# The mixing product of a hybrid decoder block as seven products of quarters, in three passes, with its weights' sums made during the convolution's output product

## The chip, the cores and the metric

The kernel runs on one core of a Trainium2 chip. The core's engines are TensorE (PE in the profile: matrix products; PEld its loading of the stationary operand), VectorE (DVE), ScalarE (ACT), GpSimd (POOL) and SyncE (SP). All DMAs of this kernel are issued from SP's queue. The metric is the device time of one execution, in microseconds, as the median of several runs of the same program.

## The reference

One decoder block for 512 tokens of width 1024, all in float32. Two token mixers run beside each other, are weighted by gates and added, and go through a mixing product; a gated feed-forward network follows. Cut to what matters:

```python
h = rmsnorm(x, norm1_g)
z_glu, z_rx, z_rg, z_ga, z_gb = split(h @ w_in + b_in)
u = z_glu[..., :1024] * sigmoid(z_glu[..., 1024:])
u = silu(layernorm(causal_depthwise_conv(u, conv_dw_w, conv_dw_b)))
y_a = u @ conv_w_out + conv_b_out
hb = rg_lru(causal_depthwise_conv(z_rx, lru_conv_w, lru_conv_b), ...)
y_b = (hb * gelu(z_rg)) @ lru_w_out
m = sigmoid(z_ga) * y_a + sigmoid(z_gb) * y_b
x = x + m @ w_mix_out                  # the mixing product, 512 x 1024 x 1024
h = rmsnorm(x, norm2_g)
x = x + (silu(h @ ffn_w1) * (h @ ffn_w3)) @ ffn_w2     # inner width 2816
return rmsnorm(x, norm_f_g)
```

## The kernel before

Up to `m` the channels lie on the 128 partitions and the 512 tokens along the free dimension. From the mixing product on, tokens lie on the partitions: four token tiles of 128, each in two halves of 512 columns.

**Every product in three matmuls.** Operands are split into a high part, rounded to TensorE's fp32r format, and a low part, the remainder (`split_to`, L106): ScalarE writes the high part (a CAST, L108 in the profile), another engine subtracts (L104). A product is high x high + high x low + low x high: `mm3` (L310, matmuls at L319) for products with channels on the partitions, `token_mm` (L676, matmuls at L680) for the mixing product, and `product` (L789, matmuls at L794) for the last one.

**Weights.** All weights are streamed in the order of one list of chunks, written with `wchunk` (L121). A chunk of up to 128x1024 is loaded by SP into one of four slots (`raw`, `RAW = 4`) and split into one of five (`hl`, `HL = 5`); its low part is made by GpSimd for the input, LRU-output, convolution-output and mixing weights, and by VectorE for the feed-forward weights. `weights(key)` (L150) emits the program for the chunks up to four places beyond the one it returns (`AHEAD = 4`). A `raw` slot comes free when both parts are made, an `hl` slot when the last matmul that reads it is done.

**Order.** But for the start, the order on each engine is set by the framework's scheduler: it goes through the program with its own estimate of the times and gives each engine the earliest instruction in program order that is ready. A tile is placed when a slot of its kind is free. On the chip each engine then executes its list strictly in that order. SP's list too: a DMA that waits for its data or its slot holds up those behind it.

**The stages around the change**, in order of time:
1. `yb`: the LRU's output product, 8 column blocks; the gate `sgb` is multiplied in.
2. `ya`, the convolution's output product ("conv_out" below), 8 blocks of 24 matmuls with weights `co0` to `co7`. After each block VectorE adds the bias, multiplies the gate (L668), adds the LRU's share (L669), and splits the result into `m{j}` (512 columns).
3. `mx`, the mixing product: 8 row blocks of `w_mix_out`. The first four blocks (`mx0` to `mx3`) are multiplied for all 8 token-and-half combinations into 8 PSUM banks. The last four (`LAST = 4`) are kept in long-lived tiles, and `mix_rows(t)` (L703) finishes token tile after token tile: 24 matmuls, the residual `x2` added (L707), the sum of squares and its root (`rstd_of`, L330), the scaled rows `xs` (L711), and `x2` stored to DRAM (L712) for the end.
4. `turn_half(hf)` (L344): `xs` of two token tiles are turned by TensorE (16 transposes, `th`, L351), and copied as high parts `h2..h` by ScalarE (L354) and low parts `h2..l` by VectorE (L355). Half 0 is written in the program before `mix_rows(3)`, half 1 among the first FFN products.
5. `f`, the FFN: 22 pairs of products with `w1` and `w3` (4 chunks for two inner blocks); the first two blocks (`EARLY = 2`) are made token half by token half. `ffn_out` (L732) multiplies and, for each second block, makes the operands of the last product (`pair_out`, L744) and the sums of its weights (`weight_sums`, L757).
6. `r`, the last product, by Strassen's scheme in Winograd's form: the 512 x 2816 operand and the 2816 x 1024 weights are cut into quarters (256 tokens x 1408, 1408 x 512), and seven products of sums of quarters take the place of eight. The sums of the weights (`t1` to `t4`) are made once on VectorE from two 512 KB loads (`ws`) and stored to DRAM; they come back as chunks. Three passes over the inner blocks follow: A with products `r1`, `r2`, `r5`; B with `r7`, `r1` continued, and `r2` anew (named `r3`); C with `r1` continued. Between passes VectorE adds the banks into the four token tiles; `finish` normalises and stores rows.

The sums of the operands that the passes need are written by `pair_out` as `ua` (split at once), `s1p`, `ea` and `va` (both split late, in pass A).

Of the kernel before, what the change touches and what calls it, by code (L numbers as in the profile page):

```python
# [75 lines left out]
def tile_block(ctx, tc, a, out):  # L76
# [139 lines left out]
    KH = NF // 2  # L216
    PAIRED = [j for k in range(KH) for j in (k, k + KH)]
    for j in PAIRED:
# [4 lines left out]
    w2 = a["ffn_w2"][0].rearrange("(k p) n -> p k n", p=P)  # L223
    b11, b12, b21, b22 = (lambda k, i=i, h=h: w2[:, k + KH * i, h * T : (h + 1) * T] for i in range(2) for h in range(2))
    dram = ctx.enter_context(tc.tile_pool(name="dram", bufs=1, space=bass.MemoryType.DRAM))
    sums_ = {(n, k): dram.tile([P, T], F32, tag=f"{n}_{k}", name=f"{n}_{k}") for n in ("t1", "t2", "t3", "t4") for k in range(KH)}
    x2_kept = [[dram.tile([P, T], F32, tag=f"x2k{t}{h}", name=f"x2k{t}{h}") for h in range(2)] for t in range(NT)]

    def quarters(key, of):
        def load(raw):  # L230
            for i, q in enumerate(of):
                nc.sync.dma_start(raw[:, i * T : (i + 1) * T], q)

        wchunk(key, load, len(of), T, lo=vec)

    two = lambda q, k: [q(i) for i in (k, k + 1) if i < KH]
    kept = lambda n: lambda k: sums_[n, k][:, :]
    for n, q, m in (("A", [b11, kept("t1")], b21), ("B", [kept("t2"), kept("t3")], b22)):
        for k in range(KH):
            if k % 2 == 0:  # L240
                quarters(f"o{n}s{k}", two(m, k))
            quarters(f"o{n}{k}", [v(k) for v in q])
    for k in range(0, KH, 2):
        quarters(f"oC{k}", two(kept("t4"), k))
# [417 lines left out]
    m = []  # L662
    for j in range(8):
        ws = w_tiles(f"co{j}", ND)
        ps = bank(f"ya{j}")
        mm3(ps, ws, un)
        o = sga[j]
        vec.scalar_tensor_tensor(out=o, in0=ps, scalar=pc("conv_b_out", j), in1=o, op0=ALU.add, op1=ALU.mult)  # L668
# [4 lines left out]
    def token_banks(name):  # L673
        return [[(bank if t < 3 else bank2)(f"{name}{t}{h}") for h in range(2)] for t in range(NT)]

    def token_mm(po_, n_k, k, x_, w_, t, h):  # L676
        xh, xl = (v[:, t * P : (t + 1) * P] for v in x_[k])
        wh, wl = w_[h]
        for i, (l_, r_) in enumerate(((xh, wh), (xh, wl), (xl, wh))):
            pe.matmul(po_[t][h], l_, r_, start=k == 0 and i == 0, stop=k == n_k - 1 and i == 2)  # L680

    def w_halves(key):
        w_ = weights(key)
        if isinstance(w_, list):
            return w_
        return [tuple(v[:, 0, h * T : (h + 1) * T] for v in w_) for h in range(2)]
# [6 lines left out]
    pm = token_banks("mx")  # L693
    for k in range(8 - LAST):
        w_ = w_halves(f"mx{k}")
        for t in range(NT):
            for h in range(2):
                token_mm(pm, 8, k, m, w_, t, h)
    wm = [w_halves(f"mx{k}") for k in range(8 - LAST, 8)]
    h2p = [pairt(f"h2{c}") for c in range(ND)]  # L700
    xs = []

    def mix_rows(t):  # L703
        for h in range(2):
            for i in range(LAST):
                token_mm(pm, 8, 8 - LAST + i, m, wm[i], t, h)
            vec.tensor_tensor(out=x2[t][h], in0=pm[t][h], in1=x2[t][h], op=ALU.add)  # L707
        sc = [longt(f"xs{t}{h}") for h in range(2)]
        r = rstd_of(x2[t], sc)
        for h in range(2):  # L710
            vec.tensor_scalar(out=sc[h], in0=x2[t][h], scalar1=r, scalar2=None, op0=ALU.mult)  # L711
# [15 lines left out]
    add = lambda o, x, y: vec.tensor_tensor(out=o, in0=x, in1=y, op=ALU.add)  # L727
    LO, HI = HALVES
    ops = []
    uv = []  # L730

    def ffn_out(j, p1, p3):  # L732
# [3 lines left out]
        if i == 0:  # L736
            uv.append((longt(f"ua{k}"), longt(f"va{k}")))
        for dst, cs in zip(uv[k], HALVES):
            vec.tensor_tensor(out=dst[:, HALVES[i]], in0=s_[:, cs], in1=p3[:, cs], op=ALU.mult)  # L739
        if i:  # L740
            pair_out(k, *uv[k])
            weight_sums(k)
# [66 lines left out]
    for k in range(KH):  # L809
        if k % 2 == 0:  # L810
            m_ = pairs_of(f"oAs{k}")
# [115 lines left out]
```

## Time and profile before

| | |
|---|---|
| median of 3 runs | 823.18 us (822.99 to 823.85) |
| the profiled execution | 823.95 us, span 821.4 us |
| TensorE busy | 810.8 us (99%), 3774 matmuls |
| VectorE, ScalarE, GpSimd busy | 556.5, 412.3, 215.4 us |
| conv_out stage (`ya`) | 377.15 to 420.83 us |
| mixing product (`mx`), with the first turning | 420.83 to 466.36 us |
| FFN (`f`), with the second turning | 466.36 to 709.81 us |
| last product (`r`) | from 709.81 us |
| DMA | 122.96 MB, mean 150 GB/s |

How to read it: times in lists are in us from the span's start, and the second number is a duration. "x168" is a count. In square brackets or after "|" stands how long the engine was idle before, and what ended that. A matmul's own duration (0.39 us) is longer than the pitch at which matmuls follow each other. In tables by stage each engine's busy time is followed by its count of instructions, and the last three columns are the clock granted to TensorE, the share of time in which the DMA engines were busy, and what they moved. `hl_co`, `hl_mx`, `hl_f` are split weights of the convolution's output, the mixing product and the FFN, `raw_..` the loaded ones.

### The profile page before, as it was taken

The numbers are of one execution on the slowest core, as the hardware profiler recorded it, in microseconds if no ns is written. First come the engines' busy times: TensorE is split into PE (matmuls) and PEld (weight loads), VectorE is DVE, ScalarE is ACT, GpSimd is POOL, SyncE is SP. The second block draws the span as 40 slices with busy tenths as digits, with TensorE's granted clock in tenths as the row PEclk, the third lists the DMA queues.
The fourth block names the chain that finished last, engine by engine and source line by source line (L and its number), as shares of the span: only waits on it lengthen the run. The fifth ranks groups of instructions, "written<-read, shape, count | busy, mean of one in ns | idle before, by whom it ended". The sixth has DMA issues, their size and how long they took to land.

```text
span 821.4 us, 10487 instructions
## 1 busy us (share of the span) xinstructions
PE 810.8 (99%) x3774; PEld 678.1 (83%) x3774; DVE 556.5 (68%) x849; ACT 412.3 (50%) x574; POOL 215.4 (26%) x120
## 2 busy tenths in 40 slices
PE   8999999999999999999999999999999999999996
PEld 7988888888888888888888898888888888888885
DVE  4699999999989965723644546554554445688457
ACT  7545788768578565733234343222222222476434
POOL 3555446445434543365461000000000000000000
PEclk9999999999999999999999999999999999999999
DMA  7544434334333412244367218666666665786552
GB/s 214 160 116 103 116 92 117 97 104 122 103 90 103 119 48 81 81 150 139 98 196 220 77 44 266 203 204 177 184 193 201 194 205 195 243 275 207 182 167 103
DMA packets 154310, 122.96 MB, mean 150 GB/s; under 512 B 10919, under 2 KB 128083, under 8 KB 154259
## 3 DMA queue, kind: packets, MB, share of 16 engines
q1 hardware_dynamic: 154259, 122.31, 49.4%
q8 instruction: 29, 0.48, 0.2%
q14 instruction: 22, 0.18, 0.1%
HBM read 103.54 MB, written 15.73 MB: 145 GB/s over the span
## 4 chain that ended last, share of the span: by engine, by line
PE 97%; ACT 1%; DMA 1%; DVE 1%; issue 0%; SPq 0%; ACTq 0%
PE z L319 34%; PE f L319 29%; PE r L794 13%; PE yb L319 7%; PE mx L680 5%; PE ya L319 5%; PE g L590 3%; DMA raw_in<-in_w_in_dram 1%; PE th L351 0%; PE tx L351 0%; DVE x L366 0%; SPq L275 0%; DVE x2b L727 0%; DVE of L859 0%; ACT hl_in L108 0%
## 5 line engine op out<-in xcount | busy, mean ns | idle before, releaser
L469 DVE SCALAR_TENSOR_TENSOR cv<-u,par,cv 128x511 f32<-128x511 f32 (+17 forms) x240 | 162.7, 730 | 1.4 <-ACT cv L466 1.2
L104 POOL TENSOR_TENSOR hl_in<-raw_in,hl_in 128x1024 fp32r<-128x1024 f32 x52 | 125.5, 2417 | 135.7 <-ACT hl_in L108 122.2
L108 ACT CAST hl_f<-raw_f 128x1024 fp32r<-128x1024 f32 x44 | 46.3, 1053 | 149.3 <-PE f L319 83.1
L104 DVE TENSOR_TENSOR hl_f<-raw_f,hl_f 128x1024 fp32r<-128x1024 f32 x44 | 53.8, 1222 | 49.2 <-ACT hl_f L108 49.2
L108 ACT CAST hl_in<-raw_in 128x1024 fp32r<-128x1024 f32 x52 | 54.2, 1043 | 11.1 <-PE z L319 6.8
L739 DVE TENSOR_TENSOR ua<-si,f 128x256 f32<-128x256 f32 x22 | 9.3, 422 | 62.9 <-PE f L319 62.2
L319 PE MATMUL z<-h10h,hl_in 128*128 128x512 f32 (+1 forms) x112 | 42.2, 378 | 0.7 <-DVE h10l L355 0.7
L319 PE MATMUL z<-h11h,hl_in 128*128 128x512 f32 (+1 forms) x112 | 41.7, 374 | 0.0
L319 PE MATMUL z<-h17h,hl_in 128*128 128x512 f32 (+1 forms) x112 | 41.7, 374 | 0.0
L319 PE MATMUL z<-h14h,hl_in 128*128 128x512 f32 (+1 forms) x112 | 41.7, 374 | 0.0
L319 PE MATMUL z<-h15h,hl_in 128*128 128x512 f32 (+1 forms) x112 | 41.7, 374 | 0.0
L319 PE MATMUL z<-h13h,hl_in 128*128 128x512 f32 (+1 forms) x112 | 41.7, 374 | 0.0
L319 PE MATMUL z<-h16h,hl_in 128*128 128x512 f32 (+1 forms) x112 | 41.7, 374 | 0.0
L319 PE MATMUL z<-h12h,hl_in 128*128 128x512 f32 (+1 forms) x112 | 41.7, 374 | 0.0
L319 PE MATMUL f<-h22h,hl_f 128*128 128x512 f32 (+1 forms) x96 | 35.4, 371 | 0.0
L319 PE MATMUL f<-h25h,hl_f 128*128 128x512 f32 (+1 forms) x96 | 35.4, 372 | 0.0
L319 PE MATMUL f<-h23h,hl_f 128*128 128x512 f32 (+1 forms) x96 | 35.4, 372 | 0.0
L319 PE MATMUL f<-h26h,hl_f 128*128 128x512 f32 (+1 forms) x96 | 35.4, 372 | 0.0
L319 PE MATMUL f<-h24h,hl_f 128*128 128x512 f32 (+1 forms) x96 | 35.4, 371 | 0.0
L319 PE MATMUL f<-h27h,hl_f 128*128 128x512 f32 (+1 forms) x96 | 35.3, 371 | 0.0
L319 PE MATMUL f<-h20h,hl_f 128*128 128x512 f32 (+1 forms) x96 | 35.0, 373 | 0.3 <-ACT h20h L354 0.3
L319 PE MATMUL f<-h21h,hl_f 128*128 128x512 f32 (+1 forms) x96 | 35.3, 371 | 0.0
(815 smaller groups left out, 2252.1 us busy)
## 6 DMA issues: line engine op xcount, KB each, us to landing
raw_in<-in_w_in_dram SPq DMA_DIRECT2D x52, 512.0 KB
raw_f<-in_ffn_w_dram SPq DMA_DIRECT2D x44, 512.0 KB
ws<-in_ffn_w_dram SPq DMA_DIRECT2D x22, 512.0 KB
t<-ws SPq DMA_DIRECT2D x44, 256.0 KB
raw_oB<-t SPq DMA_DIRECT2D x22, 256.0 KB
raw_lo<-in_lru_w_out_dram SPq DMA_DIRECT2D x16, 320.0 KB
x<-in_x_dram SPq DMA_DIRECT2D x16, 256.0 KB
raw_co<-in_conv_w_out_dram SPq DMA_DIRECT2D x8, 512.0 KB
```

Source lines behind the costliest of these rows:

```text
L104: eng.tensor_tensor(out=o, in0=x, in1=y, op=ALU.subtract)
L108: copy(h, full)
L319: pe.matmul(ps, l, r, start=i == 0, stop=i == n - 1)
L469: vec.scalar_tensor_tensor(out=acc[c][:, s:], in0=u[c][:, : T - s], scalar=dw(c, s), in1=acc[c][:, s:], op0=ALU.mult, op1=ALU.add)
L590: pe.matmul(ps, l, r, start=k == 0, stop=k == len(mms) - 1)
L680: pe.matmul(po_[t][h], l_, r_, start=k == 0 and i == 0, stop=k == n_k - 1 and i == 2)
L739: vec.tensor_tensor(out=dst[:, HALVES[i]], in0=s_[:, cs], in1=p3[:, cs], op=ALU.mult)
L794: pe.matmul(banks[i], l_[:, ts], r_, start=start and n == 0, stop=stop and n == 2, skip_group_check=again)
```

## The change

The scheme of the last product is put into two classes, `Quartered` (the chunks) and `Sevenfold` (operands and passes), and used for both the mixing product (four inner blocks a quarter) and the last one (eleven).

- conv_out's blocks are made in the order 0, 4, 1, 5, 2, 6, 3, 7. Each result is added straight into `u`/`v` tiles (two half-width additions); the split of `m` is gone. After each second block `pair` makes and splits operands, and `weight_sums` loads two row blocks of `w_mix_out` (512 KB each), makes four sums on VectorE and stores them in DRAM.
- The mixing weights no longer come as eight chunks, four of them in long-lived tiles, but as 14 chunks of quarters and sums through the five `hl` slots (As0, A0, A1, As2, A2, A3, Bs0, B0, B1, Bs2, B2, B3, C0, C2, each of two 256 KB loads), with the low part made by VectorE. The first FFN chunks follow after them in the list.
- The product is three passes: A and B of 72 matmuls, C of 24. Token tiles 0 and 1 are complete after pass B and go through `norm2_rows` ahead of pass C in the program; then stand the sums of tiles 2 and 3, then pass C: its first two blocks for both tiles, the last two (`hold` = 2) for tile 2 with its norm, then for tile 3. Only then comes `turn_half(0)`.
- In the last product, `finish` of tiles 0 and 1 now stands right after their sums, ahead of the sums of tiles 2 and 3, instead of inside pass C; `hold` stays 3.

The core of the diff:

```diff
-    for j in range(8):
+    for j in [0, 4, 1, 5, 2, 6, 3, 7]:
         wchunk(f"co{j}", conv_out[:, :, j * P : (j + 1) * P], ND, P)
-    LAST = 4
-    mix = a["w_mix_out"][0].rearrange("(k p) (o n) -> p k o n", p=P, o=1)
-    for k in range(8):
-        wchunk(f"mx{k}", mix[:, k, :, :], 1, D, "hl" if k < 8 - LAST else "long")
+    class Quartered:
+        def __init__(self, name, w, kh, lo):
...
+            for n, q, m in (("A", [raw(0, 0), kept("t1")], raw(1, 0)), ("B", [kept("t2"), kept("t3")], raw(1, 1))):
+                for k in range(kh):
+                    if k % 2 == 0:
+                        chunk(f"{n}s{k}", two(m, k))
+                    chunk(f"{n}{k}", [v(k) for v in q])
+            for k in range(0, kh, 2):
+                chunk(f"C{k}", two(kept("t4"), k))
...
+    mixq = Quartered("mx", a["w_mix_out"][0].rearrange("(k p) n -> p k n", p=P), ND // 2, vec)
...
+    class Sevenfold:
...
+        def tile(self, j, make):
+            k, i = j % self.kh, j // self.kh
+            if i == 0:
+                self.uv.append((longt(f"{self.name}u{k}"), longt(f"{self.name}v{k}")))
+            for dst, cs in zip(self.uv[k], HALVES):
+                make(cs, dst[:, HALVES[i]])
+            if i:
+                self.pair(k, *self.uv[k])
+                self.weight_sums(k)
+        def pair(self, k, ua, va):
+            n = self.name
+            u_ = split(f"{n}us{k}", ua, vec)
+            s1 = shortt(f"{n}s1{k}")[:, LO]
+            add(s1, va[:, LO], va[:, HI])
+            sp = longt(f"{n}s1p{k}", F32R)
+            split_to(sp[:, LO], sp[:, HI], s1, vec)
+            e = longt(f"{n}e{k}")
+            sub(vec, e[:, HI], ua[:, LO], va[:, LO])
+            sub(vec, va[:, LO], s1, ua[:, LO])
+            sub(vec, e[:, LO], ua[:, HI], va[:, LO])
+            self.ops.append((u_, sp, e, va))
+        def weight_sums(self, k):
+            q = [raws.tile([P, 1024], F32, tag="raw", name=f"{self.name}ws{k}_{i}") for i in range(2)]
+            for i, v in enumerate(q):
+                nc.sync.dma_start(v, self.q.w[:, k + self.kh * i, :])
+            (q11, q12), (q21, q22) = ((v[:, :T], v[:, T:]) for v in q)
+            sub(vec, q22, q22, q12)
+            sub(vec, q12, q12, q11)
+            add(q11, q22, q11)
+            sub(vec, q21, q21, q11)
+            for n, v in (("t1", q12), ("t2", q11), ("t3", q22), ("t4", q21)):
+                nc.sync.dma_start(self.q.sums[n, k][:, :], v)
...
+        def run(self, sums, begun, first_rows, last_rows, hold):
...
+            for i in range(2):
+                add(sums[i][1], q[i], sums[i][1])
+                add(sums[i][1], r2[i], sums[i][1])
+                first_rows(i)
+            for i in range(2):
+                add(sums[2 + i][1], q[i], sums[2 + i][1])
+                for h in range(2):
+                    add(sums[2 + i][h], r7[i], sums[2 + i][h])
+            held_ = []
+            for k in range(kh):
+                if k % 2 == 0:
+                    m_ = self.pairs_of(f"C{k}")
+                args = (quarter(late[k][1], HI), m_[k % 2])
+                if k < kh - hold:
+                    for i in range(2):
+                        self.product(r1, i, *args, False, False, True)
+                else:
+                    held_.append(args)
+            for i in range(2):
+                def rest():
+                    for c, args in enumerate(held_):
+                        self.product(r1, i, *args, False, c == hold - 1, True)
+                    add(sums[2 + i][0], r1[i], sums[2 + i][0])
+                last_rows(2 + i, rest)
...
-        vec.tensor_tensor(out=o, in0=o, in1=yb[j], op=ALU.add)
-        m.append(split(f"m{j}", o, vec))
+        m7.tile(j, lambda cs, dst: add(dst, o[:, cs], yb[j][:, cs]))
...
-    for t in range(3):
-        mix_rows(t)
+    m7.run(x2, lambda: None, norm2_rows, norm2_rows, 2)
     turn_half("th", xs, "norm2_g", h2p, 0, [bank])
-    mix_rows(3)
...
-        if k < 2:
-            finish(k, 0)
...
+    o7.run(x2, loads, finish, finish, 3)
```

The left-out parts of `run` are passes A and B of the last product as they were, with names that carry the product's.

More of the change, by code (lines that the diff above doesn't have):

```diff
@@ L664, in tile_block @@
+    m7 = Sevenfold(mixq)
+    for j in mixq.order():
         ws = w_tiles(f"co{j}", ND)
@@ L847, in tile_block, with loads @@
-    for i in range(2):
-        add(x2[i][1], q[i], x2[i][1])
-        add(x2[2 + i][1], q[i], x2[2 + i][1])
-        add(x2[i][1], r2[i], x2[i][1])
+    def loads():
+        for t in range(NT):
+            for h in range(2):
+                nc.sync.dma_start(x2[t][h], x2_kept[t][h][:, :])
         for h in range(2):
-            add(x2[2 + i][h], r7[i], x2[2 + i][h])
-    def finish(t, h, rest=None):
+            nc.sync.dma_start(gf[h], a["norm_f_g"][h * T : (h + 1) * T].partition_broadcast(P))
@@ L856, in finish @@
+    def finish(t, rest=None):
+        h = 1 if rest else 0
         o = [shortt(f"of{t}{i}") for i in range(2)]
```

221 lines of the change are left out of this document (72 added, 149 removed).

## The prediction

> **What bounds the kernel now.** I read the page's busy shares first, then the chain of waits in order of time, then busy time by stage.
>
> ```profile
> PE 810.8 (99%) x3774; PEld 678.1 (83%) x3774; DVE 556.5 (68%) x849; ACT 412.3 (50%) x574; POOL 215.4 (26%) x120
> ```
> ```profile
> 420.83 38.09 PE mx L680 x168
> 458.92 1.31 PE th L351 x12
> ...
> 462.46 3.90 PE mx L680 x17
> 466.36 11.52 PE f L319 x96
> ...
> 478.13 0.48 ACT h20h L354
> ...
> 709.81 102.69 PE r L794 x453
> ```
> ```profile
> core 0: us, PE busy (x) PEld busy (x) DVE busy (x) ACT busy (x) POOL busy (x), PEclk, DMA share, GB/s
> 377.15:420.83 43.68, 43.68 (x194) 36.19 (x193) 25.63 (x22) 12.79 (x15) 20.70 (x9) 1.00 0.32 99
> ...
> 799.50:814.50 15.00, 15.00 (x67) 12.11 (x65) 13.56 (x25) 8.61 (x20) 0.00 (x0) 1.00 0.19 70
> ```
>
> TensorE sets the time: it is busy for 99% of the span, and around the change the chain is nothing but matmuls, with one short wait (0.48 us, at the second half of the normalised rows, 478.13). So a matmul fewer is a gain of its full pitch, and any new wait of TensorE is a loss of its full length. One matmul of 128x512 costs 38.09/168 = 0.227 us, one of 256 columns 11.52/96 = 0.12 us. The stage windows are conv_out (377 to 421) and the third pass of the last products (799.5 to 814.5), in which VectorE (DVE) is already busy 13.56 of 15 us. The clock is 1.00 in both, so nothing here hangs on throttling. The sum below is made on the profiled execution (823.95 us, span 821.4); the median of the three runs is 823.18, 0.77 less, and the same difference is taken off at the end.
>
> **The change, part by part.** (1) *Fewer matmuls.* Before: 8 row blocks x 4 token tiles x 2 halves x 3 = 192. After: 7 quarter products x 4 blocks x 2 token tiles x 3 = 168. Saved: 24 x 0.227 = 5.44 us, all on the path, if TensorE stays fed.
>
> (2) *More for VectorE while conv_out runs.* Each pair of `m` tiles now brings four sums, a split of 512 columns and the sums of the weights.
>
> ```profile
> 382.79 0.75 DVE L668 SCALAR_TENSOR_TENSOR sga<-ya,par,sga 128x512 f32<-128x512 f32 x1 [4.75 <-PE ya L319]
> 383.96 2.56 POOL L104 TENSOR_TENSOR hl_co<-raw_co,hl_co 128x1024 fp32r<-128x1024 f32 x1 [3.06 <-ACT hl_co L108]
> 384.95 2.12 DVE L104 TENSOR_TENSOR m0l<-sga,m0h 128x512 fp32r<-128x512 f32 x1 [0.69 <-ACT m0h L108]
> 423.04 0.69 DVE L104 TENSOR_TENSOR m7l<-sga,m7h 128x512 fp32r<-128x512 f32 x1 [0.69 <-ACT m7h L108]
> ```
> ```profile
> L104 DVE TENSOR_TENSOR ws<-ws,ws x22: 684/691/693, 490.8 to 702.9; 128x512 f32<-128x512 f32 x22
> ```
> ```profile
> 515.21 1.22 DVE L104 TENSOR_TENSOR hl_f<-raw_f,hl_f 128x1024 fp32r<-128x1024 f32 x1
> 516.35 0.68 DVE L104 TENSOR_TENSOR ua1l<-ua,ua1h 128x512 fp32r<-128x512 f32 x1
> ...
> 517.28 0.41 DVE L104 TENSOR_TENSOR ea<-ua,va 128x256 f32<-128x256 f32 x1
> ```
>
> For two tiles of conv_out (10.9 us of TensorE): two readings of the product 1.5, four additions of 256 columns 1.7, the pair's split 0.68 and five half-width operations 2.1, four weight sums 2.8; 8.7 us. Four pairs make 35 us, and the four weight chunks whose low part moves from GpSimd to VectorE in this stage (1.22 each) 4.9: 40 of the stage's 43.7 us, where all that VectorE had was 25.6. It fits, just. It hides under conv_out's matmuls, which wait only for a bank, and the first pass needs the last pair only at its fourth block, 3 x 18 x 0.227 = 12.2 us in. In the first pass VectorE has five chunks (6.1), eight splits (5.5) and four additions (2.8), 14.4 of 16.3 us, so a backlog is not worked off quickly. Bounds for what TensorE waits there: 0 (the last products run passes of the same density, chain row 709.81, without a wait) and 4 us (rival two). I take 0.5, near the first, which is the same code.
>
> Beside that trace: a tensor-with-tensor operation of VectorE takes 2.12 us while GpSimd subtracts (383.96 to 386.52) and 0.69 when it does not. [...]
>
> (3) *DMA and its queue.* Removed are 8 loads of 512 KB; added 8 loads of 512 KB for the sums, 16 stores and 28 loads of 256 KB: 44 more issues on SP.
>
> ```profile
> 421.00:437.00 16.00, 16.00 (x73) 13.23 (x72) 4.46 (x5) 7.87 (x12) 10.05 (x8) 1.00 0.93 285
> ```
> ```profile
> L767 SPq DMA_DIRECT2D t<-ws x44: 319/326/700, 491.5 to 703.6; - x44
> ```
>
> At 0.33 us an issue that is 15 us of a queue over 80 us. In conv_out's 43.7 us about 7 chunks, 7 to 8 loads for sums and 16 stores pass, 11.8 MB or 270 GB/s; the row shows 285 GB/s at a share of 0.93. By my estimate from the split slots (a slot comes free every 5.44 us, with a conv_out tile) a chunk is loaded some 5 us before its turn, so I charge nothing; if that cover is gone it is part of rival two. On SP the stores wait for VectorE's sums and the next loads stand behind them, as already in the FFN stage, which has no wait on TensorE.
>
> (4) *The way out of the mixing product, where the cover goes.* Before, the sums, norms and weight splits lie apart: the first five FFN chunks are split early, and rows of the fourth tile (24 matmuls) run while the first half of `h2` is turned.
>
> ```profile
> 433.61 1.23 DVE L104 TENSOR_TENSOR hl_f<-raw_f,hl_f 128x1024 fp32r<-128x1024 f32 x1 [9.88 <-ACT hl_f L108]
> ...
> 443.76 1.22 DVE L104 TENSOR_TENSOR hl_f<-raw_f,hl_f 128x1024 fp32r<-128x1024 f32 x1 [2.55 <-ACT hl_f L108]
> ...
> 451.40 0.15 DVE L341 RECIPROCAL stats<-stats 128x1 f32<-128x1 f32 x1
> 451.58 0.88 DVE L711 TENSOR_SCALAR xs<-x,stats 128x512 f32<-128x512 f32 x2
> ...
> 461.35 0.48 DVE L355 SCALAR_TENSOR_TENSOR h21l<-th,par,h21h 128x256 fp32r<-128x256 f32 x1
> 461.75 0.88 DVE L711 TENSOR_SCALAR xs<-x,stats 128x512 f32<-128x512 f32 x2
> 462.54 0.48 DVE L355 SCALAR_TENSOR_TENSOR h22l<-th,par,h22h 128x256 fp32r<-128x256 f32 x1
> 462.93 0.48 DVE L355 SCALAR_TENSOR_TENSOR h23l<-th,par,h23h 128x256 fp32r<-128x256 f32 x1
> 463.32 0.48 DVE L355 SCALAR_TENSOR_TENSOR h24l<-th,par,h24h 128x256 fp32r<-128x256 f32 x1
> 463.71 0.68 DVE L707 TENSOR_TENSOR x<-mx,x 128x512 f32<-128x512 f32 x1
> ```
>
> These rows also show VectorE's order: what is ready goes by its place in the program (the norm of the third tile, 461.75, ahead of ready low parts of `h2`; the fourth tile's sum, written later, only in a gap).
>
> After, the mix weights hold the five split slots to the end, so four FFN chunks are split around the third pass; the sums there are 14 instead of 8, and none of them is ready before the last 3.2 us of the second pass; and nothing stands between the third pass and the FFN but the turning. Let E be the end of the second pass. The third pass is 24 matmuls, to E+5.44. The same sums in the last products show what VectorE does with them:
>
> ```profile
> 796.40 0.68 DVE L727 TENSOR_TENSOR q<-r,q 128x512 f32<-128x512 f32 x1
> 797.00 1.22 DVE L104 TENSOR_TENSOR hl_oC<-raw_oC,hl_oC 128x1024 fp32r<-128x1024 f32 x1
> 798.13 0.68 DVE L727 TENSOR_TENSOR q<-r,q 128x512 f32<-128x512 f32 x1
> 798.73 0.68 DVE L727 TENSOR_TENSOR x2b<-q,x2b 128x512 f32<-128x512 f32 x1
> 799.33 1.23 DVE L104 TENSOR_TENSOR hl_oC<-raw_oC,hl_oC 128x1024 fp32r<-128x1024 f32 x1
> 800.47 0.68 DVE L727 TENSOR_TENSOR x2b<-q,x2b 128x512 f32<-128x512 f32 x1
> 801.07 1.88 DVE L727 TENSOR_TENSOR x2b<-r,x2b 128x512 f32<-128x512 f32 x3
> 802.87 1.28 DVE L727 TENSOR_TENSOR x2b<-q,x2b 128x512 f32<-128x512 f32 x2
> 804.07 1.88 DVE L727 TENSOR_TENSOR x2b<-r,x2b 128x512 f32<-128x512 f32 x3
> ```
>
> There the second pass ends at 709.81 + 396 x 0.227 = 799.5, so the twelve sums and two weight splits run from E-3.1 to E+6.4 without a break: 9.5 us, of which the splits are 2.3 (797.00 to 798.13 is one) and a sum 0.60. They cost nothing there because 66 matmuls of the third pass cover them. In the mixing product the third pass is 5.44 us long, and ahead of the first low part of `h2` in the program stand those 9.5 us, two more FFN splits (2.3), the norms of two tiles (2 x 1.05) and the last sums of the other two (1.2): 15.1 us, from E-3.1 to E+12.0. Then come eight low parts at 0.39 (461.75 aside, the pitch of 462.54 to 463.32) with the other two norms (2.1) among them: the last is there at E+17.2, and TensorE is through the first FFN product's first half at E+17.4. With operands at hand it would be there at 5.44 + 16 transposes of 1.31/12 (1.75) + 24 x 0.12 (2.88) = E+10.1. TensorE loses 7.3 us. ScalarE's squares, casts and high parts run beside this and are charged nothing.
>
> ```profile
> L108 ACT CAST hl_f<-raw_f 128x1024 fp32r<-128x1024 f32 x44 | 46.3, 1053 | 149.3 <-PE f L319 83.1
> ```
>
> Bounds of this term: 1 us if only what the low parts need is ahead of them (eight sums less, one or two splits less; the copies of the first chunk alone stay open), and 10 us if two or three of ScalarE's casts (1.05 each) fall between squares and norms. I take 7.3, since the sums' own row is the nearest and the order is shown.
>
> (5) *The last products* keep their matmuls; two `finish` calls move ahead of the sums of the other tiles, under the 15 us of the third pass. No more than 0.3 us either way: taken as 0, since the last additions wait for TensorE in both.
>
> Sum: 823.95 - 5.44 + 0.5 + 7.3 = 826.3 for the profiled execution, 825.5 for the median: slower by 2.3 us, 0.3%. A measurement of this kernel tells 0.2% (1.65 us) from no change.
>
> **The rivals.** *One: the gain stays (other side).* One mechanism: VectorE turns `h2`'s low parts before the sums of the last two tiles and the later FFN splits. For it: those are not needed before, and the rows at 461 to 464 show fine interleaving. Against: the order seen there goes by the program. Price: six sums (3.6) and two splits (2.3) leave the 7.3, so 1.4 remain: 823.18 - 5.44 + 1.4 = 819.1. It decides from the point where 1.9 us or more of the backlog moves behind (5.44 is then no longer eaten up).
>
> *Two: VectorE and DMA fall behind already in conv_out.* 40 of 43.7 us leaves 3.7, and the three GpSimd splits could take 7.7 of it by the 2.12 row: a backlog of 4 us, of which the first pass works off 1.9. TensorE then waits at the first pass's last block and where the second pass reuses the first product's bank, for about 3.5 us: 829. Against: the first stretch has few sums yet, and each need lies 4 to 12 us behind its source. [...]
>
> *Three: it cancels.* The two later FFN splits fall behind the low parts (their loads are late on SP), the rest as forecast: 7.3 - 2.3 = 5.0, and 823.2 - 5.44 + 5.0 + 0.5 = 823.3.
>
> That the product would not get cheaper in matmuls has no place: 168 against 192 is counted in the code.
>
> **How the numbers follow.** Forecast (loss of 6 to 9 us at the turning) 0.48, rival one 0.25, two 0.15, three 0.12. The forecast's own range is 823.9 to 828. Leaving out a tenth at each end: low 819.5 inside rival one, high 829. Faster by over 0.2% (under 821.5): rival one, 0.25. Within: rival three and the forecast's lower edge, 0.12 + 0.08 = 0.20. Slower: 0.55.
>
> **What would show it.** Right: 168 matmuls of the mixing product at 0.227; a wait of TensorE on VectorE's low parts of `h2` just after the third pass, 5 us or more in all, with VectorE busy without a gap through it on sums and FFN splits; no wait of over 1 us in conv_out and the first two passes. Wrong: TensorE going from the third pass into the FFN with a wait of 1 to 2 us (rival one), or waits on weight chunks, stores or bank readings before the second pass (rival two). What I trust least is the place of the FFN splits in that window: 1.14 us each, four of them.

## The result, and the profile after

The changed kernel takes 834.23 us (median of four runs, 833.12 to 836.13) against 823.18: slower, ratio 1.0135 with a 95% interval of 1.0115 to 1.0155. The profiled execution took 836.13 us with a span of 834.3, 12.9 us more than the span of before. Its page gives the busy time of each engine:

```profile
PE 813.2 (97%) x3750; PEld 678.4 (81%) x3750; DVE 591.5 (71%) x921; ACT 420.8 (50%) x586; POOL 195.8 (23%) x108
```

The 24 matmuls are gone (3774 to 3750), yet TensorE is busy 2.4 us longer: it must have run slowly somewhere, and besides that it now stands still. The waits of TensorE from conv_out to the FFN (engine, line and what it waited for: us in total, times, longest), first before, then after:

```profile
PE f L319 <- ACT h20h L354: 0.3, 1, 0.3
```
```profile
PE th L355 <- DVE x L666: 2.8, 2, 2.7
PE mxr L727 <- DVE sga L801: 2.5, 1, 2.5
PE mxr L727 <- ACT hl_mxB L108: 2.3, 1, 2.3
PE th L355 <- DVE xs L818: 1.9, 2, 1.0
PE mxr L727 <- DVE hl_mxB L104: 0.8, 1, 0.8
```

So three places wait: pass A (`sga`, the reading of a conv_out bank), the start of pass B (its first weights), and the turning (`th`). Busy time by stage shows a further loss (busy us and count of PE, PEld, DVE, ACT, POOL, then the granted clock, the DMA share and GB/s):

```profile
core 0: us, PE busy (x) PEld busy (x) DVE busy (x) ACT busy (x) POOL busy (x), PEclk, DMA share, GB/s
...
421.50:441.00 19.50, 16.95 (x74) 13.44 (x73) 15.04 (x25) 6.78 (x10) 0.00 (x0) 1.00 0.77 265
441.00:451.00 10.00, 6.98 (x18) 5.22 (x18) 8.54 (x11) 5.55 (x7) 0.00 (x0) 0.66 0.85 287
...
469.20:478.80 9.60, 4.73 (x21) 2.51 (x20) 9.56 (x21) 5.46 (x17) 0.00 (x0) 0.78 0.61 191
478.80:491.70 12.90, 12.89 (x98) 12.89 (x99) 2.83 (x7) 2.43 (x7) 0.00 (x0) 0.90 0.12 49
```

In the 10 us from the start of the stop ahead of pass B the granted clock is 0.66, in the turning 0.78 and after it 0.90. TensorE's own rows show the pitch (start, duration, line, what, count):

```profile
445.65 1.05 PE L727 MATMUL mxr<-hl_mxB,mxeb0h 128*128 128x512 f32 x2
446.50 0.63 PE L727 MATMUL mxr<-hl_mxB,mxeb0l 128*128 128x512 f32 x1
...
451.39 0.39 PE L727 MATMUL mxr<-hl_mxB,mxvb0l 128*128 128x512 f32 x1
451.62 0.40 PE L727 MATMUL mxr<-hl_mxB,mxeb1h 128*128 128x512 f32 x1
```

Two matmuls from 445.65 to 446.50 are 0.43 us each; from 451.39 to 451.62 it is 0.23. From 444.63 on 14 matmuls of pass B ran at about half speed (an expectation below speaks of 17); the granted clock from 444.60 to 450.69 is 0.51. Ahead of them TensorE had stood for 2.26 + 0.76 us with one matmul between; behind the single stop of 2.55 us in pass A the clock was 1.00 (427.88 to 440.94).

What stands behind the three places is seen in the chain of waits (start, us, what), which in the kernel before was nothing but matmuls here:

```profile
417.92 4.94 DMA raw_mxA<-mxt
...
426.46 2.93 DMA mxt<-mxws
...
430.79 6.05 DMA x<-in_x_dram
436.85 5.32 DMA raw_mxB<-mxt
442.27 1.05 ACT hl_mxB L108
443.35 1.24 DVE hl_mxB L104
444.63 19.19 PE mxr L727 x71
...
470.18 0.87 DVE xs L818 x2
471.06 2.27 DVE hl_f L104 x2
473.39 1.19 DVE x L666 x2
474.58 1.13 DVE hl_f L104
475.84 0.87 DVE xs L818 x2
476.71 0.39 DVE h20l L359
...
478.81 12.86 PE f L323 x96
```

Store of a sum, eight loads of `x`, load of the sum, split, matmul: the weights of pass B came straight off this queue. VectorE's list shows the stop in pass A and the order at the turning:

```profile
422.61 0.69 DVE L104 TENSOR_TENSOR mxws<-mxws,mxws 128x512 f32<-128x512 f32 x1 [2.62 <-DMA raw_mxA<-in_w_mix_out_dram]
...
427.08 0.74 DVE L801 SCALAR_TENSOR_TENSOR sga<-ya,par,sga 128x512 f32<-128x512 f32 x1
...
459.53 1.23 DVE L104 TENSOR_TENSOR hl_f<-raw_f,hl_f 128x1024 fp32r<-128x1024 f32 x1 [1.54 <-ACT hl_f L108]
...
463.67 1.21 DVE L104 TENSOR_TENSOR hl_f<-raw_f,hl_f 128x1024 fp32r<-128x1024 f32 x1
...
470.97 2.35 DVE L104 TENSOR_TENSOR hl_f<-raw_f,hl_f 128x1024 fp32r<-128x1024 f32 x2
...
476.62 0.48 DVE L359 SCALAR_TENSOR_TENSOR h20l<-th,par,h20h 128x256 fp32r<-128x256 f32 x1
```

VectorE stood idle for 2.62 us in front of a sum whose load had not come, and the last reading of conv_out (427.08, of a bank that was complete when conv_out's matmuls ended at 421.76) stood behind it in its list. TensorE, which needs that bank, waited until 427.88.

The account of the stretch from the first matmul of the mixing product to the first transpose after the first FFN half is 57.04 us before and 69.76 after. The parts: the 24 matmuls, -5.44; pass A, 421.76 to 440.94 instead of 72 x 0.227 = 16.3, +2.8; the stop ahead of pass B to 443.37, +2.4; pass B to 463.64, 20.27 instead of 16.3, +3.9, of which 0.76 is the second wait and the rest half speed; pass C, turning and the first FFN half 28.0 instead of 5.44 + 1.75 + 11.52 = 18.7, +9.3. In these 9.3, the transposes end 7.8 us late (9.59 us from 469.22 to 478.81 instead of 1.75) and the FFN's 96 matmuls take 12.86 instead of 11.52 at the lower clock. Ahead of the FFN now stand 20 transposes and not 16; four of them belong to the second half. The sum is +13.0, against 12.7 measured; before, too, the stretch was some 0.2 us longer than its matmuls at these pitches. Outside it the product starts 1.1 later, and this delay is there already at the start of the LRU's output product (323.37 instead of 322.27), ahead of the changed stages. The rest of the FFN, whose second turning is shorter, takes 1.1 less.

### The profile page after: what moved, and what is told of

The parts are those of the page before. It is cut to its first block, busy times and chain, and to the rows that moved or that the text cites. A ratio compares the mean times of both kernels' runs of the same rounds, so it can differ in the third digit from the quotient of the medians.

```text
span 834.3 us, 10605 instructions
## 1 busy us (share of the span) xinstructions
PE 813.2 (97%) x3750; PEld 678.4 (81%) x3750; DVE 591.5 (71%) x921; ACT 420.8 (50%) x586; POOL 195.8 (23%) x108
## 4 chain that ended last, share of the span: by engine, by line
PE 89%; DVE 5%; DMA 4%; issue 1%; ACT 1%; SPq 0%; DVEq 0%; ACTq 0%
PE z L323 34%; PE f L323 29%; PE or L727 12%; PE yb L323 7%; PE g L594 3%; PE mxr L727 2%; PE ya L323 1%; DMA raw_mxA<-mxt 1%; DMA raw_in<-in_w_in_dram 1%; DMA x<-in_x_dram 1%; DMA raw_mxB<-mxt 1%; DVE mxws L104 1%; DVE x L666 0%; DVE sga L801 0%; DVE hl_f L104 0%
## 5 line engine op out<-in xcount | busy, mean ns | idle before, releaser
L831 DVE TENSOR_TENSOR ou<-si,f 128x256 f32<-128x256 f32 x22 | 9.3, 421 | 63.5 <-PE f L323 62.9
```

Of the source, the lines that this page charges most:

```text
L831: o7.tile(j, lambda cs, dst: vec.tensor_tensor(out=dst, in0=s_[:, cs], in1=p3[:, cs], op=ALU.mult))
```

## The experiments

The theory after this result: three causes add up, (a) a feed that is starved in conv_out and pass A by the loop load, sum on VectorE, store, reload, with the loads of `x` pushed into it; (b) half speed after the stop ahead of pass B; (c) at the turning, VectorE's list. Rivals: that VectorE's work alone is too much, that DMA throughput alone is, or that the turning costs it all. Beside the times each run has one stretch of its trace: from the first matmul of the mixing product to the first transpose after the first FFN half (before 57.04 us, after 69.76; with nothing lost it would be 57.04 - 5.44 = 51.6).

| run | median us | ratio to before (95%) | stretch us |
|---|---|---|---|
| `x` loaded early | 829.18 | 1.0058 (1.0041 to 1.0075) | 64.01 |
| sums early | 827.10 | 1.0035 (1.0020 to 1.0050) | 61.42 |
| turning first | 832.38 | 1.0097 (1.0079 to 1.0114) | 66.36 |
| all three | 824.60 | 1.0006 (0.9997 to 1.0015) | 57.35 |
| no sums on VectorE | 826.32 | 1.0031 (1.0020 to 1.0042) | 60.62 |
| no stores | 828.36 | 1.0049 (1.0035 to 1.0063) | 62.56 |
| matmuls that keep TensorE busy | 835.64 | 1.0149 (1.0135 to 1.0162) | 71.21 |
| FFN splits on GpSimd | 835.45 | 1.0139 (1.0123 to 1.0154) | 72.03 |
| all three, `r7` late | 822.10 | 0.9979 (0.9970 to 0.9987) | 55.85 |
| sums early, `r7` late | 824.39 | 1.0006 (0.9997 to 1.0015) | 58.50 |
| all three, `r7` late, two chunks ahead | 818.86 | 0.9937 (0.9924 to 0.9951) | 52.55 |

**The loads of `x` ahead of conv_out's third block.**

```diff
-    for j in mixq.order():
+    for n, j in enumerate(mixq.order()):
+        if n == 2:
+            x2 = [...]      # the eight loads, moved from behind conv_out
```

> The changed kernel, but the eight loads of x for the residual (2 MB) are issued within conv_out, before its third block, instead of behind the last sums of the weights. Theory F (feed: these loads stand on SP ahead of the chunks of t2 and t3 that the second pass needs): the second pass starts without the 2.3 us wait at 443, and without the half-rate matmuls after it (17 at 0.427 instead of 0.227 us, 3.4 us): 5 to 6 us faster than the changed kernel, about 828.5. Theory T (turn: the loss is VectorE's backlog behind the third pass alone): within 1 us of the changed kernel, 833 to 835. The wait at 427 and the loss behind the third pass (9 us) stay in both.

Measured: 829.18 us, 5.05 less than the change as it was. Pass B starts at 439.05 without a wait for its weights; two waits stay in passes A and B, 0.9 us for `sga` and 1.2 for a sum. Where the loads of `x` stand is thus worth about 5 us, more than the 3 us for which TensorE stood ahead of pass B: the half speed behind that stop goes with it (0.23 us a matmul through both passes). Not all of it lies there. Pass A takes 17.47 us instead of 19.18, so its wait, which was expected to stay, is shorter by 1.7 as well.

**The weights' sums during the LRU's output product.**

```diff
+    for j in range(8):                       # yb, moved behind Sevenfold
...
+        if j % 2 == 0:
+            m7.weight_sums(j // 2)
...
-                self.weight_sums(k)          # in tile(), now for the last product alone
```

> The changed kernel, but the sums of the mixing weights (loads, VectorE, stores) are made during the LRU's output product, one stage earlier, instead of in conv_out. Theory F: the wait of 2.5 us in the first pass's first block (VectorE stands behind a sum that waits for its load) goes, and the chunks of the second pass come earlier since the DMA queue has 8 MB less in that stage: 3 to 8 us faster than the changed kernel, 826 to 831. Theory T: the same within 1 us. A rival: the LRU's output product loses what conv_out gains, since GpSimd splits its weights without a pause and VectorE's sums contend with it; then that stage (47.6 us from 330 on) gets longer.

Measured: 827.10 us, 7.1 less. The waits of TensorE in the window are two, and its busy time by stage is full to the end of pass C:

```profile
PE th L355 <- DVE x L658: 2.7, 1, 2.7
PE th L355 <- DVE xs L822: 1.9, 2, 1.0
```
```profile
421.50:441.00 19.50, 19.50 (x87) 16.14 (x87) 17.68 (x27) 12.51 (x18) 0.00 (x0) 1.00 0.77 269
```

The whole feed loss of the change (2.8 + 2.4 + 3.9) disappears when the loop load, sum, store lies one stage earlier. The rival that the LRU's output product pays for it did not happen: from its first matmul to conv_out's it is 54.88 us here, in the change and before. The turning is untouched: from the end of pass B (453.77) to the end of the first FFN half (482.51) it is 28.7 us, 10.0 over 18.7.

**The turning ahead of the last sums and of pass C in the program.**

```diff
                 first_rows(i)
+            if turned:
+                turned()
...
-    m7.run(x2, lambda: None, norm2_rows, norm2_rows, 2)
-    turn_half("th", xs, "norm2_g", h2p, 0, [bank])
+    m7.run(x2, lambda: None, norm2_rows, norm2_rows, 2, lambda: turn_half("th", xs, "norm2_g", h2p, 0, [bank]))
```

> The changed kernel, but the turning of the first two token tiles stands in the program ahead of the sums of tiles 2 and 3 and of the third pass. Theory T: VectorE makes the first low part of h2 at about 6.5 us behind the end of the second pass instead of 13, TensorE goes into the FFN some 6 us earlier: 5 to 7 us faster than the changed kernel, about 828. Theory F: no more than 1 us faster. The waits at 427 and 443 stay in both.

Measured: 832.38 us, 1.9 less; the expectation was too high. In this run pass A waited 3.2 us for `sga`, longer than the 2.5 before, and half speed followed (nine matmuls in 3.84 us from 429.51 on, 0.43 each). B began with waits of only 0.3 and 0.8 us and without half speed, and its end came only 1.5 us earlier (462.15). From there to the end of the first FFN half 25.5 us, 6.8 over 18.7 instead of 9.3: the transposes now wait for their banks, which VectorE must read (`th` waits 1.3 and 0.9 us for the low parts `h20l` and `h21l`, 0.8 for `xs`). The order in the program alone moves a part of the loss; VectorE is still late. Since the feed differs too, the 1.9 us are not the price of the order alone.

**All three.** The three edits above in one kernel:

```diff
+        if n == 2:                            # x early
+            m7.weight_sums(j // 2)            # sums early, in yb
+            if turned:                        # turning first
```

> All three at once: x loaded early, the weights' sums one stage earlier, the turning ahead of the other tiles' sums. If the two causes are separate and together the whole loss, the gain of 24 matmuls (5.44 us) appears but for 1 to 2 us at the turning: 818.5 to 820.5, faster than the kernel before (823.2). If the passes have a further bound (VectorE or DMA as such), 823 to 826.

Measured: 824.60 us, as long as before; the 818.5 to 820.5 of two separate causes did not come. The feed has no wait at all; the turning loses 6.0 us (453.35 to 478.06). So the sum of the single gains (5.05 + 7.1 + 1.9) is not what the kernel gains (9.6): the first two repair the same loss. What is left is cause (c), and it eats the 5.44 us.

**What starves the feed: VectorE's sums, or the stores.** Two kernels that leave work out.

```diff
-            sub(vec, q22, q22, q12)            # and the three other sums
+            if self.name != "mx":
+                sub(vec, q22, q22, q12)
```

> The changed kernel without the sixteen VectorE operations that make the sums of the mixing weights (the plain quarters are stored and used in their place, so the mixing product is another one); their loads, stores and chunks stay. What starves the first two passes is either VectorE's 11 us of sums in conv_out or the DMA traffic and its queue. VectorE: the waits at 427 and 443 go, 5 to 8 us faster than the changed kernel, 826 to 829. DMA: the wait at 443 stays within 1 us of what it was (2.3 us and the half-rate matmuls behind it), and only the wait at 427 goes, 2 to 3.5 us faster, 831 to 832.

```diff
-                nc.sync.dma_start(self.q.sums[n, k][:, :], v)
+                if self.name != "mx":
+                    nc.sync.dma_start(self.q.sums[n, k][:, :], v)
...
-            kept = lambda n: lambda k: self.sums[n, k][:, :]
+            kept = ...                         # plain quarters of w_mix_out for "mx"
```

> The changed kernel without the sixteen stores of the mixing weights' sums; the chunks that would bring them back load plain quarters of the weights of the same size, so the mixing product is another one. Loads and VectorE's sums stay. DMA: 4 MB less in conv_out and no chunk behind a store; the second pass starts without its wait: 4 to 7 us faster than the changed kernel, 827 to 830. VectorE: both waits stay, less than 1.5 us faster.

Measured: 826.32 and 828.36 us. Each alone takes nearly the whole feed loss away: no wait of TensorE over 0.3 and 0.8 us before the turning. Stage rows of the stretch that is 16.95 us busy in the change, first without the VectorE sums, then without the stores:

```profile
421.50:441.00 19.50, 19.22 (x86) 15.59 (x85) 17.14 (x26) 12.26 (x17) 0.00 (x0) 1.00 0.95 336
```
```profile
421.50:441.00 19.50, 18.68 (x82) 15.15 (x82) 17.13 (x27) 11.74 (x17) 0.00 (x0) 1.00 0.97 335
```

The DMA engines move 336 GB/s here against 265 in the change, so they were not at their limit; and VectorE does more in this stretch (17.1 us against 15.0), in the second kernel with all its sums, and was busy for only 33.4 of conv_out's 43.5 us in the change, so it wasn't either. Each run came out as expected for the one resource that it relieves, VectorE or DMA; that both did speaks against either alone. What the two kernels have in common is that the loop is broken: without the sums a store waits for no VectorE, without the stores no load stands behind one (and no chunk waits for a sum, which that edit frees as well). The waits of SP's queue in the change between 400 and 450, and of VectorE between 376 and 450, show the loop:

```profile
SPq L716 <- DMA mxws<-in_w_mix_out_dram: 7.5, 2, 4.1
SPq L716 <- DVE mxws L104: 5.1, 6, 2.4
```
```profile
DVE mxws L104 <- DMA raw_mxA<-in_w_mix_out_dram: 6.1, 2, 3.5
DVE mxws L104 <- POOL hl_co L104: 2.9, 1, 2.9
```

SP stands with a store that waits for the sum, the sum waits for its load, and the next load stands behind the store. Half of this alone does little harm. Without the sums SP's stores still wait 13.1 us for their loads between 400 and 450, but VectorE, with its splits and bank readings, no longer stands behind a load. Without the stores VectorE still waits 5.9 us for the loads of its sums, but in four pieces, and no store holds up the queue behind them. That the two `raw` slots a `weight_sums` holds until its last store has read them take part is likely, since there are four of them; no run shows it alone.

**Matmuls that keep TensorE busy between passes A and B.**

```diff
+            if n == "mx":
+                wp = bank2("warm2")
+                for _ in range(16):
+                    pe.matmul(wp, self.ops[kh - 1][0][0][:, :P], self.ops[kh - 1][0][0], start=True, stop=True)
```

> The changed kernel, with 16 more matmuls of 512 columns into a spare bank, whose result nobody reads, between the first and the second pass (3.6 us at full rate). If the half-rate matmuls behind the wait at 443 come from TensorE having been idle, the second pass starts at 0.227 us a matmul and the 16 lie inside the wait: 2.5 to 3.5 us faster than the changed kernel, about 831, and the granted clock in that stretch is 0.95 or more instead of 0.66. If the slow matmuls come from something else (operands, banks, DMA traffic), they stay slow and the 16 cost up to 1 us: 834 to 835.

Measured: 835.64 us, not faster than the change. The mechanism shows, the time doesn't (times by stage, as above):

```profile
429.67:433.08 3.41, 3.28 (x8) 2.60 (x9) 3.25 (x7) 1.02 (x2) 0.00 (x0) 0.50 0.75 270
...
441.00:451.00 10.00, 10.00 (x45) 8.03 (x44) 8.15 (x12) 6.84 (x10) 0.00 (x0) 1.00 0.95 327
```

The clock in the 10 us that had 0.66 is 1.00, and pass B takes 16.56 us (448.03 to 464.59) instead of 20.27. From the end of pass A (444.40) to that of B it is 20.2 us against 22.7, so the dummies buy 2.5. But in this kernel the wait of pass A for `sga` is 4.1 us instead of 2.5, and this time half speed follows it (the first row): pass A takes 22.25 us instead of 19.18, which takes all of the gain back. From the end of pass B to the end of the first FFN half another 0.9 us is lost. Why the wait is longer with an edit that lies behind it is not shown. That half speed follows from the stop is shown; what it costs by itself is only bounded by these 2.5 us and the 3.1 of the account (3.9 less the wait of 0.76).

**The first four FFN chunks' low parts on GpSimd.**

```diff
-    for j in ff_order:
+    for n, j in enumerate(ff_order):
+        lo = pool_e if n < 2 else vec
```

> The changed kernel, but the low parts of the first four FFN chunks are made by GpSimd, which is idle there, instead of by VectorE: four operations of 1.14 us leave VectorE's backlog behind the second pass. Theory T as predicted (VectorE's backlog in program order, each operation at its pitch): first low part of h2 some 4 us earlier, 3 to 4.5 us faster than the changed kernel, 830 to 831. [...] Rival (ScalarE's norms set the turning, not VectorE): under 1 us.

Measured: 835.45 us, nothing gained, though 4 x 1.22 us left VectorE. Its rows, GpSimd's first and then VectorE's:

```profile
463.67 2.41 POOL L104 TENSOR_TENSOR hl_f<-raw_f,hl_f 128x1024 fp32r<-128x1024 f32 x1 [1.64 <-DVE x L667]
468.40 4.85 POOL L104 TENSOR_TENSOR hl_f<-raw_f,hl_f 128x1024 fp32r<-128x1024 f32 x2 [2.32 <-ACT hl_f L108]
```
```profile
464.30 2.33 DVE L667 TENSOR_TENSOR x<-mxq,x 128x512 f32<-128x512 f32 x1
469.07 4.46 DVE L819 TENSOR_SCALAR xs<-x,stats 128x512 f32<-128x512 f32 x2
```

A sum of 0.68 us takes 2.33 and two scalings, 0.88 together without GpSimd, take 4.46; they end 0.55 and 0.28 us behind GpSimd's operations. The first low part is at 478.27, later than in the change (476.62). What VectorE is spared it loses in standing. The scaling, of one tensor by a column, was held up as well as the sum of two tensors.

**`r7` in a pass of its own behind B.** Added to the three edits: the product `r7`, needed only by tiles 2 and 3, leaves pass B for a pass D of 24 matmuls between B (then 48) and C. Tiles 0 and 1 are complete 24 matmuls earlier, and more of their sums, norms and turning lies beside matmuls.

```diff
-                for r in (1, 2, 0) if ends else (0, 1, 2):
+                for r in (1, 2) if own else (1, 2, 0) if ends else (0, 1, 2):
...
+            if n == "mx":
+                for k in range(kh):
...
+                        self.product(r7, i, quarter(late[k][0], HI), m_[k % 2], k == 0, k == kh - 1)
```

> The three edits of the run before together (x early, weights' sums one stage earlier, turning ahead of the other tiles' sums), and in the mixing product the product r7, which only tiles 2 and 3 need, gets a pass of its own between the second and the third: tiles 0 and 1 are complete after 48 matmuls of the second pass, and 48 matmuls (10.9 us) instead of 24 (5.44 us) cover their sums, norms and the turning. Theory T (what is left there is cover that is too short: first low part 8.5 us behind the tiles' completion against 5.44 us of matmuls): nearly the whole 5.44 us appears: 818 to 819.5, faster than the kernel before. Rival (VectorE or the bank turnover of the transposes as such): 822 to 824, as without it.

Measured: 822.10 us, 2.5 less than with the three edits alone and faster than before by 0.2%, but not the 818 to 819.5 of the theory. The FFN's first half takes 13.08 us at a granted clock of 0.87. In its chain two FFN splits still stand between the low parts:

```profile
460.37 1.13 DVE hl_f L104
461.50 0.40 DVE h22l L364
461.90 0.48 DVE hl_f L104
```

**`r7` late and sums early, without the two others.** The edits of these two diffs on the changed kernel.

```diff
+            m7.weight_sums(j // 2)
...
+                        self.product(r7, i, quarter(late[k][0], HI), m_[k % 2], k == 0, k == kh - 1)
```

> Two edits only: the weights' sums one stage earlier, and r7 of the mixing product in a pass of its own behind the second. No early x, no early turning. If the turning ahead of the other tiles' sums matters only as long as the cover is short, this is within 1 us of the version with all four edits, 822 to 823. If VectorE's order still counts (the backlog in program order is 12 us against 10.9 us of matmuls), it is 1.5 to 3 us slower, 823.5 to 825.

Measured: 824.39 us, 2.7 less than with the sums early alone. Early `x` and the early turning are then worth 2.3 us more (822.10).

**The same as 822.10, with the weights emitted two instead of four chunks ahead in passes D and C.** This moves the FFN's splits behind the low parts in the program, and so in VectorE's list.

```diff
-            h, l = weights(self.name + key)
+            h, l = weights(self.name + key, 2 if self.name == "mx" and key[0] in "CD" else AHEAD)
```

> The version with all four edits, and in the last two passes of the mixing product the weights are emitted two chunks ahead instead of four, so the splits of the first FFN chunks stand behind the turning in the program. Theory T (in that version the transposes wait twice, 2 us, for low parts of h2 that stand behind FFN splits on VectorE): 0.8 to 2 us faster than it, 820 to 821.3. Rival: the FFN weights come too late instead and the first FFN matmuls wait: 822 to 824.

Measured: 818.86 us (818.08 to 820.50), ratio 0.9937 (0.9924 to 0.9951): faster than both kernels, by 5.0 and 15.4 us. All that TensorE waits for from conv_out to the FFN, and the chain at the turning:

```profile
PE th L360 <- DVE x L663: 0.3, 1, 0.3
PE f L328 <- ACT h20h L363: 0.3, 1, 0.3
```
```profile
454.85 0.44 PE th L360 x4
455.29 1.62 PE mxr L725 x7
...
461.38 1.42 PE f L328 x10
...
462.82 10.57 PE f L328 x86
```

That is more than the 0.8 to 2 us expected. Transposes lie among the matmuls of the last pass, and the FFN's first half takes 11.85 us at full clock, 1.2 less than in the run of 822.10. The stretch is 52.55 us, 0.95 over what it would be without any loss.

## Why the prediction was right and wrong

*The direction was right, the time wrong:* 834.23 against 825.5, and beyond the end of the range at 829. On the profiled executions the forecast was 826.3 and 836.13 came, 9.8 more (this execution is itself 1.9 over the median of its runs). Of these, 8.6 are the feed (9.1 measured, 0.5 taken) and 2.0 the turning. The later start adds 1.1, the second turning takes 1.1 off, the last stage and the time outside the span 0.6; together 10.0, which is too much by the 0.2 of the account above. With the feed whole (sums early) the kernel takes 827.10, 1.6 over the forecast of 825.5.

*Step 1, fewer matmuls:* right. 3750 instead of 3774; where the feed is whole, a pass of 72 matmuls takes 16.32 us (sums early), which is 0.227 each.

*Step 2, VectorE in conv_out, is where the prediction failed* ("I take 0.5, near the first"). The stage itself lost nothing, 43.5 us in both, as forecast, and VectorE was not too slow for it: it was busy for 33.4 us of it, where 40 were forecast. But the bound of 4 us was drawn for work that lies back to back. VectorE did not work back to back: it waited for the loads of its own sums, once in a way that held TensorE in pass A. "The same code" in the last products is no near row for this, since there the sums were made a stage earlier, among the FFN; putting them a stage earlier here removed the whole loss.

*Step 3, DMA, failed with it* ("so I charge nothing"). The cover of some 5 us was worked out from slots and not from the queue. Left out were the eight loads of `x`, which stand in the program behind conv_out and so, on SP's list, in the middle of pass B's weights: 6 us of queue, and 5 us of time by the run that moved them. The comparison of 270 with 285 GB/s looked at the wrong limit: the engines reached 336 GB/s when the loop was broken.

*That "nothing here hangs on throttling" was wrong.* It read the clock of the kernel before, which had no stops (its one wait of TensorE is 0.3 us; the forecast's 0.48 is the ScalarE copy that ended it). A stop of 3 us gave about 3 us more at half speed, and the turning 1.3 in the FFN. A forecast that lets TensorE wait for 3 us at one place must, by this case, add what the clock takes afterwards: here the wait of 3.0 us was followed by 3.1 us of loss at a clock of 0.51.

*Step 4, the turning, had the right mechanism and was sized 2.0 us too small.* First low part forecast at the end of pass B + 12.0, measured + 13.0 (463.64 to 476.62); VectorE was busy for 9.56 of 9.60 us (469.20 to 478.80), with sums, norms and, from 459.5 on, five FFN splits instead of four. Of the loss of 9.3, 7.8 lie ahead of the FFN and 1.3 are the lower clock, which had no term. Two details came otherwise. TensorE stood in the transposes and not behind them, 2.8 us until the sums `x` were made and 1.9 for scaled rows. And ScalarE, "charged nothing", made the first high part at 476.06, 5 us after its transposes: in its list the squares of a later tile stood ahead, and they waited 3.0 us for VectorE's sum.

*Step 5, the last products:* right, 111.6 us from their first matmul to the end before, 111.7 after.

*Rival one* did not happen here, yet its price held when it was built, with more edits than it had named: "1.4 remain", 819.1 us; the version with a whole feed and the low parts ahead of later splits has 0.95 left and takes 818.86. That the times agree this closely is partly luck, since the feed, `r7` and the early `x` are in no term of it. *Rival two* did happen in its substance, VectorE and DMA behind already in conv_out, with 2.5 and 3.0 us of waiting for its "about 3.5", but by another path: not in pass A's last block but in its first, for a bank, and at the start of pass B for weights. VectorE was held up beside GpSimd's splits in conv_out: three operations took 2.13, 2.50 and 2.22 us instead of 0.42, 0.42 and 0.69, and each ended 0.3 to 0.6 us behind the end of a split. That is 5.3 us more in all; the 7.7 named, three times the 2.56 us of a split, were an estimate and no run shows them. Since VectorE afterwards stood 6.1 us for loads, it was not short of time; how much these operations delayed the loop is not shown. And it came on top of the forecast and not in its place. The two were given as cases that exclude each other (0.48 and 0.15) though nothing ties the feed in conv_out to the list at the turning. Added up, as independent terms, they would have given 825.5 + 3.5 = 829 already without the clock. *Rival three* did not happen: the FFN splits were not late.

*What would show it:* the wait at the turning with VectorE busy through it came, though with 4.7 us instead of "5 us or more" and for `x` and `xs`; "no wait of over 1 us in conv_out and the first two passes" did not.

## What to carry to other kernels

Where a stage gets work that runs load, compute, store and reload through one in-order queue and a few slots, busy shares say little: follow one item round the loop and list everything else that the queue issues between its parts; breaking the loop, by starting it a stage earlier, was worth 7 us here. Causes at different places are terms of a sum and no rivals, and a stop of TensorE can cost more than its length: behind each of the four stops of 3.0 to 4.1 us in passes A and B the matmuls followed at 0.43 instead of 0.23 us, behind the two of 2.55 and 2.71 us at 0.23. A saving at the end of a product is had only if what follows is ordered so that the next stage's first operand comes first: here it took the reordering of the last passes and later weight splits to turn +1.35% into -0.63%.

## What the runs showed of the hardware that was not expected

- A stop of TensorE of 2.26 + 0.76 us with one matmul between was followed by 14 matmuls at about 0.43 us instead of 0.23 (granted clock 0.51 over 6.1 us). With the FFN splits on GpSimd the stop there was 2.59 + 0.46 us, and the matmuls behind it came at 0.43 us as well. In pass A a stop of 3.24 us (turning first) was followed by matmuls at 0.43 us too, and with one of 4.09 us (matmuls that keep TensorE busy), which ended at 429.80, the clock was 0.50 from 429.67 to 433.08. Behind stops of 2.55 us (the change; clock 1.00) and 2.71 us (FFN splits on GpSimd) in pass A the pitch was 0.23 us. With 16 matmuls filling the gap ahead of pass B the clock was 1.00 from 441 to 451.
- While 20 transposes were spread over 9.6 us (the change, from 469.2) the clock was 0.78, and 0.90 in the FFN's 96 matmuls after them; in the first half of the FFN it was 1.00 before.
- Beside GpSimd's subtractions of 128x1024 (two in 4.85 us) VectorE's scaling of one tensor by a column was held up as well: two took 4.46 us, and 0.88 together otherwise (FFN splits on GpSimd).
